# Up-projection of a decoder block: one written order for four engines instead of the scheduler's, and other buffers for operands and weights

## The chip, the cores and the metric

The kernel runs on one core of a Trainium2 chip. The metric is device time in microseconds (us) of the program. Before the change three runs gave 2145.63 us as their median (2145.47 to 2150.24); the run that was profiled took 2145.27 us. Engines are called as the profile calls them: PE (TensorE), PEld (its weight loads), DVE (VectorE), ACT (ScalarE), POOL (GpSimd) and SP (the queue that issues the DMAs).

## The reference, cut to what matters

One decoder layer in float32, 1024 tokens, model width 1024. The change lies in the first half of the feed-forward part:

```
x = layer_norm(ALPHA*x + mixed, ln1_g, ln1_b)          # x: 1024 x 1024
h = causal_dwconv(x @ w_up, conv_w, conv_b)            # w_up: 1024 x 5632; 3 taps over tokens
h_gate, h_val = split(h, 2)                            # 2816 columns each
ffn = (silu(h_gate) * h_val) @ w_down
```

Before it stand the token mixers and the first layer norm, behind it the down-projection and a last gated stage; they compute the same in both kernels.

## The kernel before, in words

A float32 product is made of three fp32r matmuls: each operand is split into a high part (`hi_of`, L101, on ACT) and the rest (`lo_of`, L106, on POOL or DVE), and `mm3` adds high x high, high x low and low x high (L155).

The up-projection takes the 44 blocks of 128 columns of `w_up` as 22 pairs: block f of the gate half and block f of the value half. For a pair, 256 columns times 1024 tokens, the 2x2 scheme with seven products is used (Strassen-Winograd): `left_operands` makes seven operands of the weights, called W0 to W6 here, with four additions or subtractions on DVE (L164), `right_operands` made the seven XS tiles of the tokens once, before the stage. Each product is 4 x 3 = 12 matmuls of 512 columns, so a pair has 84. Products land in four PSUM banks A to D and are put together by DVE (L1043) and ACT (L1050, L1074) into two halves `h`. The convolution of a half is one ACT instruction (L1085) and two taps on DVE (L1087); the gate half goes through Silu on ACT (L1089), POOL multiplies it with the value half (L164), and SP stores it to DRAM (L1097).

The weights of pair f+1 are made while pair f is multiplied. There is one buffer for each of the seven W (four in pool `wq`, three in `fp`), so W of the next pair waits until the product of the last pair is done with it. The raw weights of even pairs lie in `wr` tiles, of odd pairs in `ar` tiles.

What sets the order: the code of a pair is a list of steps (`p0, p1, late p6, p5, late conv0, p2, p3, p4, conv1`), and the framework's scheduler, which works through a modelled timeline, orders the instructions of each engine on that base. Each engine then takes its instructions strictly in that order, each waiting for semaphores. The other stages are ordered by the scheduler in both kernels.

The last pair's gate half (`last_conv`) is finished within the first preparations of the down-projection, which are `bank_sets` of weights (`wu`) and activations (`au`).

Of the kernel before, what the change touches and what calls it, by code (L numbers as in the profile page):

```python
# [8 lines left out]
F32 = mybir.dt.float32  # L9
F32R = mybir.dt.float32r  # L10
# [7 lines left out]
P = 128  # L18
L = 1024
# [21 lines left out]
def hybrid_block(ctx: ExitStack, tc: tile.TileContext, x, p, w_in, w_gate_up, b_gate, g_gla, w_gla,  # L41
# [48 lines left out]
    def nm(s):  # L90
        uid[0] += 1
        return f"{s}_{uid[0]}"
# [15 lines left out]
    def split(hi, lo, src, eh="A", el="V"):  # L108
        hi_of(hi, src, eh)
        lo_of(lo, src, hi, el)  # L110
# [104 lines left out]
    def quad(a):  # L215
        return a.rearrange("p (a b) -> p a b", b=P)
# [39 lines left out]
    def run(steps):  # L256
        for f in steps:
            f()
# [687 lines left out]
    segd, segk = ExitStack(), ExitStack()  # L946
    xpool = pool("xset", stack=segx)
    open_residual([x[t * P:(t + 1) * P, :] for t in range(NT)], 5)
    XS = [bpool.tile([P, 2, 4, HALF], F32R, name=nm("xs"), tag="B") for _ in range(4)]
    with ExitStack() as c1:  # L950
        lp = pool("ln1", stack=c1)
        gb1 = load_gb(lp, ln1_g, ln1_b)
        SPREAD, XE, XA = (1, 3), ('GVGVGVG', 'GVGVGVG', 'GGGVGGG', 'VVGVVGV'), ('VVVV', 'VVVV', 'VVVV', 'VVVG')

        def x_sets(i, xf):

            if i == 0:
# [40 lines left out]
    with ExitStack() as c1:  # L998
        psum_banks(c1, "d", ch=8)
        fp = pool("ffwork", stack=c1)  # L1000
        rawp = pool("raws", stack=segd, side="right")
        wk = pool("upwork", stack=segk, side="right")
        UE, UE0, US = 'GGGGGGG', 'VVGVVGV', 'VVVV'
        nset = [0]

        def blocks(f):

            return (NF + f, f) if f < NF - 1 else (f, NF + f)

        def w_sets(f):  # L1010
# [8 lines left out]
            W = []  # L1019
            for _ in range(7):  # L1020
                n = nset[0] % 7
                nset[0] += 1
                pl, nb = (wq, 4) if n < 4 else (fp, 3)
                W.append([pl.tile([P, 512], F32R, name=nm(x), tag=x, bufs=nb) for x in ("wh", "wl")])
            run(left_operands(raw[1][:, :512], raw[1][:, 512:], raw[0][:, :512], raw[0][:, 512:],
                              lambda j, src: split(*W[j], src, "A", (UE if f else UE0)[j]), US))
            return [[quad(t) for t in w] for w in W]

        def up(f):

            W = w_sets(f)
            st, out_ = {}, {}

            def prod(ps, j, start):
                for k in range(4):
                    mm3(ps, (W[j][0][:, k], W[j][1][:, k]), (XS[j][:, 0, k], XS[j][:, 1, k]), start and k == 0, k == 3,
                        not start)  # L1040

            def plus(out, a, b):
                V.tensor_tensor(out=out, in0=a, in1=quad(b), op=ALU.add)  # L1043

            def p0():
                st["A"] = bank("ch")
                prod(st["A"], 0, True)
                st["h"] = [wk.tile([P, L], F32, name=nm("h"), tag=f"h{i}", bufs=2) for i in range(2)]
                st["hv"] = [h.rearrange("p (a g q) -> p g a q", g=2, q=P) for h in st["h"]]
                S.activation(st["hv"][1][:, 0], quad(st["A"]), AF.Copy)  # L1050

            def p1():
                st["B"] = bank("ch")
                prod(st["B"], 1, True)
                plus(st["hv"][0][:, 1], st["hv"][1][:, 0], st["B"])

            def p5():
                st["C"] = bank("ch")
                prod(st["C"], 5, True)

            def p2():
                st["D"] = bank("ch")
                prod(st["D"], 2, True)

            def p3():
                prod(st["B"], 3, False)
                s1, u3 = st["hv"][1][:, 0], st["hv"][1][:, 1]
                plus(u3, s1, st["B"])
                plus(s1, u3, st["C"])
                plus(u3, u3, st["D"])  # L1070

            def p4():
                prod(st["A"], 4, False)
                S.activation(st["hv"][0][:, 0], quad(st["A"]), AF.Copy)  # L1074

            def p6():
                prod(st["D"], 6, False)
                o = st["hv"][0][:, 1]
                plus(o, o, st["D"])

            def conv(i):
                c = blocks(f)[1 - i]
                h = st["h"][i]
                o = out_[c // NF] = wk.tile([P, L], F32, name=nm("cv"), tag="cv", bufs=3)
                S.activation(o, h, AF.Identity, bias=cbias[:, c:c + 1], scale=cw[:, 2, c:c + 1])  # L1085
                for d in (1, 2):
                    V.scalar_tensor_tensor(o[:, d:], h[:, :L - d], cw[:, 2 - d, c:c + 1], o[:, d:], ALU.mult, ALU.add)  # L1087
                if c < NF:
                    S.activation(o, o, AF.Silu)  # L1089

            def conv1():
                conv(1)

            def conv0():
                conv(0)
                sums(out_[0], out_[0], out_[1], ALU.mult, "G")
                nc.sync.dma_start(d_act[f // 6][:, f % 6], out_[0])  # L1097
            return p0, p1, p5, p2, p3, p4, conv1, p6, conv0

        late = []  # L1100
        for f in range(NF):
            p0, p1, p5, p2, p3, p4, conv1, *rest = up(f)
            run([p0, p1, *late[:1], p5, *late[1:], p2, p3, p4, conv1])
            late = rest
        late[0]()
        last_conv = late[1]
    segx.close()
    sega.close()

# [7 lines left out]
    with ExitStack() as c1:  # L1117
# [251 lines left out]
```

## Time and profile before

| what | value |
|---|---|
| median of the runs | 2145.63 us |
| the profiled execution | 2145.27 us, its span 2143.6 us |
| PE busy | 2063.3 us (96%) |
| DVE busy | 1564.6 us (73%) |
| POOL busy | 1000.0 us (47%) |
| ACT busy | 846.0 us (39%) |
| up-projection, first to last matmul | about 1296 to 1736 us of the span |

The profile shows, for each engine, when an instruction ran, how long, how long the engine stood idle before it and what released it. An engine's share over the whole span says little here, since the stages differ; the stage is read in stretches of its own. A pair of the up-projection repeats with the same pattern from one pair to the next, so one pair shows nearly all.

### The profile page before, as it was taken

What the parts mean: (1) busy time and instruction counts of PE and PEld (TensorE: products, weight loads), DVE (VectorE), ACT (ScalarE), POOL (GpSimd) and SP (SyncE); (2) the same over time, 40 slices, a digit from 0 to 9 for tenths busy, and PEclk for the clock granted to TensorE, in tenths of its full rate; (3) what the DMA queues carried; (4) which work ended last, traced back from release to release, by engine and by line L of the source; (5) the groups of instructions that cost most, each with busy time, mean ns of one, the idle gap of its engine ahead of it and who ended that gap; (6) DMA issues with size and microseconds to landing.
All of it is one profiled execution on the core that took longest, in us unless ns stands there. A gap on an engine that the chain in (4) does not pass through costs nothing.

```text
span 2143.6 us, 32563 instructions
## 1 busy us (share of the span) xinstructions
PE 2063.3 (96%) x12210; PEld 1811.3 (84%) x12210; DVE 1564.6 (73%) x2742; ACT 846.0 (39%) x1540; POOL 1000.0 (47%) x832
## 2 busy tenths in 40 slices
PE   9999999999999999999999978999999979999997
PEld 8888899998988888887788976877777769989897
DVE  3589999999227888876234487777777788895965
ACT  4343312213126766675222244344344353342421
POOL 2423444535422121213231586776776684554753
PEclk9999999999999999999999998999999989999999
DMA  4322211211226686779766442222222134323222
GB/s 138 79 64 79 86 31 57 57 50 52 64 86 130 130 157 130 144 158 212 205 216 122 147 153 87 86 72 87 81 69 89 64 109 148 118 94 119 89 99 79
DMA packets 377566, 227.14 MB, mean 106 GB/s; under 512 B 189328, under 2 KB 351760, under 8 KB 377408
## 3 DMA queue, kind: packets, MB, share of 16 engines
q1 hardware_dynamic: 377408, 225.06, 38.7%
q8 instruction: 96, 1.57, 0.3%
q14 instruction: 62, 0.51, 0.1%
HBM read 146.37 MB, written 40.89 MB: 87 GB/s over the span
## 4 chain that ended last, share of the span: by engine, by line
PE 29%; DVE 9%; POOL 7%; issue 5%; DMA 3%; ACT 2%; SPq 0%; POOLq 0%; DVEq 0%; ACTq 0%
PE ch L155 16%; PE mm L155 13%; POOL wl L106 4%; DVE cv L1087 1%; DMA wr<-d_ob 1%; DVE cx L164 1%; DMA dr<-in_w_down_dram 1%; DVE h L1043 1%; ACT cv L1085 1%; DVE ar L164 1%; DVE wu L106 1%; DVE res_all L910 1%; DVE res_all L164 0%; DVE stats L933 0%; POOL lnmv L212 0%
## 5 line engine op out<-in xcount | busy, mean ns | idle before, releaser
L106 POOL TENSOR_TENSOR wl<-wr,wh 128x512 fp32r<-128x512 f32 x304 | 439.8, 1461 | 288.3 <-ACT wh L101 280.7
L155 PE MATMUL ch<-xs,wh 128*128 128x512 f32 x1232 | 384.8, 394 | 5.8 <-ACT wh L101 3.2
L155 PE MATMUL mm<-Ah,wh 128*128 128x512 f32 x832 | 332.1, 399 | 2.7 <-ACT wh L101 1.6
L155 PE MATMUL mm<-Al,wh 128*128 128x512 f32 x832 | 330.4, 397 | 0.3 <-POOL Al L106 0.3
L155 PE MATMUL mm<-Ah,wl 128*128 128x512 f32 x832 | 329.4, 396 | 0.0
L155 PEld LDWEIGHTS ch<-xs,wh 128*128 128x128 f32 x1232 | 231.5, 189 | 58.7 <-DVE h L1043 4.1
L103 POOL TENSOR_SCALAR wh<-wr 128x512 fp32r<-128x512 f32 x112 | 75.2, 674 | 381.1 <-PE mm L155 194.4
L155 PE MATMUL ch<-xs,wl 128*128 128x512 f32 x616 | 242.8, 395 | 6.8 <-POOL wl L106 6.7
L155 PE MATMUL mm<-wl,Ah 128*128 128x256 f32 x768 | 217.1, 284 | 5.2 <-POOL wl L106 5.1
L155 PE MATMUL mm<-wh,Al 128*128 128x256 f32 x768 | 215.8, 283 | 0.0
L155 PE MATMUL ch<-wu,au 128*128 128x256 f32 x1512 | 194.0, 292 | 22.5 <-DVE au L106 7.2
L155 PE MATMUL mm<-wh,Ah 128*128 128x256 f32 x768 | 213.2, 283 | 0.0
L1087 DVE SCALAR_TENSOR_TENSOR cv<-h,cw,cv 128x1023 f32<-128x1023 f32 x88 | 168.6, 1915 | 60.0 <-ACT cv L1085 58.5
L155 PEld LDWEIGHTS ch<-wu,au 128*128 128x128 f32 x1512 | 190.4, 199 | 25.9 <-DVE au L106 8.1
L101 ACT ACTIVATE wh<-wr 128x512 fp32r<-128x512 f32 (+1 forms) x201 | 120.5, 623 | 194.7 <-PE mm L155 81.6
L155 PEld LDWEIGHTS mm<-Ah,wh 128*128 128x128 f32 x832 | 156.7, 188 | 33.4 <-ACT wh L101 2.1
L155 PEld LDWEIGHTS mm<-Ah,wl 128*128 128x128 f32 x832 | 156.4, 188 | 33.0
L155 PEld LDWEIGHTS mm<-Al,wh 128*128 128x128 f32 x832 | 156.5, 188 | 30.7 <-POOL Al L106 0.8
L674 DVE MATCH_REPLACE8 score<-m,score 128x896 f32<-128x896 f32 (+3 forms) x192 | 166.5, 869 | 0.0
L673 DVE MAX8 m<-score 128x8 f32<-128x896 f32 (+3 forms) x192 | 163.6, 876 | 2.3 <-POOL score L480 2.1
L155 PEld LDWEIGHTS mm<-wl,Ah 128*128 128x128 f32 x768 | 145.1, 189 | 7.1 <-POOL wl L106 6.4
L155 PEld LDWEIGHTS ch<-xs,wl 128*128 128x128 f32 x616 | 116.5, 189 | 38.2 <-POOL wl L106 14.0
(269 smaller groups left out, 4328.4 us busy)
## 6 DMA issues: line engine op xcount, KB each, us to landing
wr<-in_w_in_dram SPq DMA_DIRECT2D x60, 512.0 KB, 3.8
wr<-in_w_up_dram SPq DMA_DIRECT2D x22, 512.0 KB, 3.9
ar<-in_w_up_dram SPq DMA_DIRECT2D x22, 512.0 KB, 4.0
d_act<-cv SPq DMA_DIRECT2D x22, 512.0 KB, 2.6
dr<-in_w_down_dram SPq DMA_DIRECT2D x12, 768.0 KB, 7.0
ar<-d_act SPq DMA_DIRECT2D x12, 768.0 KB, 5.1
d_tg<-tg SPq DMA_DIRECT2D x32, 256.0 KB, 2.0
wr<-in_w_out_dram SPq DMA_DIRECT2D x16, 512.0 KB, 3.6
```

The lines of the kernel that those rows point to most:

```text
L101: S.activation(dst, src, AF.Copy, scale=scale)
L103: (V if eng == "V" else G).tensor_scalar(dst, src, scale, 0.0, ALU.mult, ALU.add)
L106: done["GV"[eng != "G"]] = (G if eng == "G" else V).tensor_tensor(out=dst, in0=src, in1=hi.bitcast(F32), op=ALU.subtract)
L155: T.matmul(ps, lhsT=l, rhs=r, start=start, stop=stop, skip_group_check=more)
L164: (G if eng == "G" else V).tensor_tensor(out=out, in0=a, in1=b, op=op)
L673: V.max(m8, score[t])
L674: V.match_replace(score[t], m8, score[t], TAKEN)
L910: V.scalar_tensor_tensor(r[:, a:b], r[:, a:b], mv[:, 2:3], gb[1][:, a:b], ALU.mult, ALU.add)
L1043: V.tensor_tensor(out=out, in0=a, in1=quad(b), op=ALU.add)
L1085: S.activation(o, h, AF.Identity, bias=cbias[:, c:c + 1], scale=cw[:, 2, c:c + 1])
L1087: V.scalar_tensor_tensor(o[:, d:], h[:, :L - d], cw[:, 2 - d, c:c + 1], o[:, d:], ALU.mult, ALU.add)
```

## The change: what it does

Four engines (PE, DVE, ACT, POOL) get a written order. Every step of a pair has a time in a plan, in microseconds from the pair's start (`ON` = 2.72 for a product, `PAIR` = 7 x `ON` = 19.04 for a pair); the steps of all pairs are sorted by that time and issued in that order, with the scheduler told to keep it. SP's order is still the scheduler's. Instructions, shapes and engines stay as they were.

Two assignments of buffers change as well. XS 5, 2, 3, 4 now lie in pool `B` and XS 0, 1, 6 elsewhere (before: 0 to 3 in `B`); W 0, 5, 1, 2 lie in `wq` and W 3, 4, 6 in `fp` (before: W 0 to 3 in `wq`, 4 to 6 in `fp`). Each W still has one buffer of its own. The last pair's value half and gate half are convolved as before, the gate half still as `last_conv`.

The diff, cut (the table of plan times shown by two lines for each kind):

```diff
-    XS = [bpool.tile([P, 2, 4, HALF], F32R, name=nm("xs"), tag="B") for _ in range(4)]
+    XS = {j: bpool.tile([P, 2, 4, HALF], F32R, name=nm("xs"), tag="B") for j in (5, 2, 3, 4)}
...
-                XS.extend(apool[0].tile([P, 2, 4, HALF], F32R, name=nm("xs"), tag="A") for _ in range(2))
-                XS.append(xpool.tile([P, 2, 4, HALF], F32R, name=nm("xs"), tag="X"))
+                for j, (pl, tag) in enumerate(((apool[0], "A"), (apool[0], "A"), (xpool, "X"))):
+                    XS[(0, 1, 6)[j]] = pl.tile([P, 2, 4, HALF], F32R, name=nm("xs"), tag=tag)
...
+        ON = 2.72
+        PAIR = 7 * ON
...
+        def w_place(j):
+            pl, nb = (wq, 4) if j in (0, 5, 1, 2) else (fp, 3)
+            return [pl.tile([P, 512], F32R, name=nm(x), tag=x, bufs=nb) for x in ("wh", "wl")]
+        plan = []
+        def at_time(t, f):
+            plan.append((t, len(plan), f))
...
+        def plan_weights(f):
+            t0 = (f - 1) * PAIR
...
+            def hi(t, j, src):
+                def f_():
+                    w[j] = w_place(j)
+                    hi_of(w[j][0], r[src], "A")
+                at_time(t0 + t, f_)
+            def lo(t, j, src):
+                at_time(t0 + t, lambda: lo_of(w[j][1], r[src], w[j][0], "G"))
+            def comb(t, out, x, y, op):
+                at_time(t0 + t, lambda: sums(r[out], r[x], r[y], op))
+            at_time(t0 - 8.0, load)
...
+            comb(6.1, "11", "11", "21", ALU.subtract)
...
+            lo(15.0, 1, "22")
...
+        def plan_pair(f):
+            t0 = f * PAIR
...
+            def store():
+                sums(st["o", 0], st["o", 0], st["o", 1], ALU.mult, "G")
+                sent[0] = nc.sync.dma_start(d_act[f // 6][:, f % 6], st["o", 0])
...
+            prod(1, "B", 1)
+            plus(5.45, (0, 1), (1, 0), "B")
...
+            last = conv(0, PAIR + 9.0, PAIR + 10.3, PAIR + 13.4) + [(t0 + 2 * PAIR + 5.5, store)]
...
+        with tc.manual_schedule(engines={nc.tensor.engine, nc.vector.engine, nc.scalar.engine, nc.gpsimd.engine}):
+            for _, _, step in sorted(plan, key=lambda e: e[:2]):
+                step()
...
-            last_conv()
+            run(last_conv)
```

What this does to the queues is small in the middle of the stage. POOL, one round, before. `wl` is the low part of a W, `cv` the multiplication of the two halves; `ar` are the raw weights of the pair in hand (its last W is W6), `wr` those of the next pair in the order W0, W5, W1, W2, W3, W4:

```order
L106 TENSOR_TENSOR wl_2515_14755<-wr_2513_14752,wh_2514_14754 128x512
L106 TENSOR_TENSOR wl_2503_14623<-ar_2489_14608,wh_2502_14622 128x512
L106 TENSOR_TENSOR wl_2525_14765<-wr_2512_14750,wh_2524_14764 128x512
L164 TENSOR_TENSOR cv_2509_14698<-cv_2509_14698,cv_2487_14602 128x1024
L106 TENSOR_TENSOR wl_2517_14757<-wr_2512_14750,wh_2516_14756 128x512
L106 TENSOR_TENSOR wl_2519_14759<-wr_2512_14750,wh_2518_14758 128x512
L106 TENSOR_TENSOR wl_2521_14761<-wr_2513_14752,wh_2520_14760 128x512
L106 TENSOR_TENSOR wl_2523_14763<-wr_2513_14752,wh_2522_14762 128x512
```

The same round on POOL in the changed kernel (here `wr` is the pair in hand and `ar` the next):

```order
L106 TENSOR_TENSOR wl_2484_14526<-ar_2470_14443,wh_2483_14525 128x512
L164 TENSOR_TENSOR cv_2465_14422<-cv_2465_14422,cv_2453_14344 128x1024
L106 TENSOR_TENSOR wl_2488_14563<-wr_2446_14299,wh_2487_14562 128x512
L106 TENSOR_TENSOR wl_2492_14583<-ar_2469_14441,wh_2491_14582 128x512
L106 TENSOR_TENSOR wl_2496_14606<-ar_2469_14441,wh_2495_14605 128x512
L106 TENSOR_TENSOR wl_2498_14610<-ar_2469_14441,wh_2497_14609 128x512
L106 TENSOR_TENSOR wl_2500_14627<-ar_2470_14443,wh_2499_14626 128x512
L106 TENSOR_TENSOR wl_2504_14649<-ar_2470_14443,wh_2503_14648 128x512
```

The multiplication has moved two places up, from just ahead of W1's low part to just behind W0's. DVE in the same round, before (`ar` and `wr` rows are the four combinations of raw weights, the first for W6 of the pair in hand, the other three for the next pair; `h` are the sums with PSUM banks, `cv` the taps):

```order
L164 TENSOR_TENSOR ar_2345_13744<-ar_2345_13744,ar_2344_13742 128x512
L164 TENSOR_TENSOR wr_2369_13888<-wr_2369_13888,wr_2368_13886 128x512
L164 TENSOR_TENSOR wr_2368_13886<-wr_2368_13886 128x512
L1043 TENSOR_TENSOR h_2361_13791<-h_2362_13792,ch_2363_13794 128x4x128
L1043 TENSOR_TENSOR h_2337_13647<-h_2337_13647,ch_2342_13697 128x4x128
L1087 SCALAR_TENSOR_TENSOR cv_2365_13834<-h_2337_13647,cw_72,cv_2365_13834 128x1023
L1087 SCALAR_TENSOR_TENSOR cv_2365_13834<-h_2337_13647,cw_72,cv_2365_13834 128x1022
L164 TENSOR_TENSOR wr_2368_13886<-wr_2368_13886,wr_2369_13888 128x512
```

And in the changed kernel:

```order
L164 TENSOR_TENSOR ar_2326_13579<-ar_2326_13579,ar_2325_13577 128x512
L1111 TENSOR_TENSOR h_2365_13822<-h_2362_13803,ch_2361_13790 128x4x128
L164 TENSOR_TENSOR wr_2350_13723<-wr_2350_13723,wr_2349_13721 128x512
L164 TENSOR_TENSOR wr_2349_13721<-wr_2349_13721 128x512
L1111 TENSOR_TENSOR h_2341_13678<-h_2341_13678,ch_2346_13705 128x4x128
L1123 SCALAR_TENSOR_TENSOR cv_2369_13846<-h_2341_13678,cw_72,cv_2369_13846 128x1023
L1123 SCALAR_TENSOR_TENSOR cv_2369_13846<-h_2341_13678,cw_72,cv_2369_13846 128x1022
L164 TENSOR_TENSOR wr_2349_13721<-wr_2349_13721,wr_2350_13723 128x512
```

The first sum with a bank has moved up by two places; all else stands as it stood. At the stage's start, the last rows of DVE ahead of the first sum with a bank, before, where XS 1 is `xs_2057`:

```order
L106 TENSOR_TENSOR xs_2059_11730<-xq_2222_12993,xs_2059_11730 128x4x128
L164 TENSOR_TENSOR wr_2225_13042<-wr_2225_13042,wr_2226_13044 128x512
L106 TENSOR_TENSOR xs_2057_11728<-xq_2224_13000,xs_2057_11728 128x4x128
L164 TENSOR_TENSOR wr_2226_13044<-wr_2226_13044,wr_2225_13042 128x512
L106 TENSOR_TENSOR wl_2230_13049<-wr_2225_13042,wh_2229_13048 128x512
L106 TENSOR_TENSOR wl_2234_13053<-wr_2226_13044,wh_2233_13052 128x512
L106 TENSOR_TENSOR wl_2240_13059<-wr_2226_13044,wh_2239_13058 128x512
```

In the changed kernel, where XS 1 is `xs_2151`:

```order
L164 TENSOR_TENSOR wr_2226_13044<-wr_2226_13044,wr_2225_13042 128x512
L106 TENSOR_TENSOR xs_2152_12439<-xq_2224_13000,xs_2152_12439 128x4x128
L106 TENSOR_TENSOR xs_2058_11729<-xq_2222_12993,xs_2058_11729 128x4x128
L164 TENSOR_TENSOR xq_2224_13000<-xq_2224_13000,xq_2217_12972 128x512
L106 TENSOR_TENSOR wl_2240_13075<-wr_2226_13044,wh_2239_13074 128x512
L106 TENSOR_TENSOR xs_2151_12438<-xq_2224_13000,xs_2151_12438 128x4x128
```

XS 1, which the second product reads, has moved from the fifth place from the end to the last.

## Rows read from the trace of the kernel before

**Rows 1.** Busy time of each engine in stretches (us, instructions in brackets), granted clock.
```profile
core 0: us, PE busy (x) PEld busy (x) DVE busy (x) ACT busy (x) POOL busy (x), PEclk, DMA share, GB/s
1322.00:1398.00 76.00, 76.00 (x337) 62.91 (x336) 57.36 (x52) 32.10 (x47) 51.23 (x30) 1.00 0.25 77
1398.00:1736.00 338.00, 331.20 (x1430) 265.68 (x1429) 245.34 (x221) 140.16 (x205) 237.89 (x136) 1.00 0.25 80
1736.00:1746.00 10.00, 4.35 (x21) 3.27 (x19) 9.96 (x14) 7.94 (x16) 8.95 (x8) 0.77 0.03 10
```

**Rows 2.** Waits from 1300 to 1736 us: who for whom, us in total, times, longest.
```profile
PE ch L155 <- POOL wl L106: 6.7, 16, 0.6
```

**Rows 3.** PE in order of time: start, us, count; in brackets idle before and releaser.
```profile
1416.24 0.61 PE L155 MATMUL ch<-xs,wh 128*128 128x512 f32 x2
1416.69 0.39 PE L155 MATMUL ch<-xs,wl 128*128 128x512 f32 x1
1416.92 0.61 PE L155 MATMUL ch<-xs,wh 128*128 128x512 f32 x2
...
1419.41 0.61 PE L155 MATMUL ch<-xs,wh 128*128 128x512 f32 x2
1420.44 0.50 PE L155 MATMUL ch<-xs,wl 128*128 128x512 f32 x1 [0.41 <-POOL wl L106]
```

**Rows 4.** POOL in order of time, one round.
```profile
1436.60 2.41 POOL L164 TENSOR_TENSOR cv<-cv,cv 128x1024 f32<-128x1024 f32 x1 [2.37 <-issue]
1438.98 6.98 POOL L106 TENSOR_TENSOR wl<-ar,wh 128x512 fp32r<-128x512 f32 x4
1445.92 1.28 POOL L106 TENSOR_TENSOR wl<-wr,wh 128x512 fp32r<-128x512 f32 x1
1448.56 1.67 POOL L106 TENSOR_TENSOR wl<-ar,wh 128x512 fp32r<-128x512 f32 x1 [1.35 <-ACT wh L101]
1452.29 1.82 POOL L106 TENSOR_TENSOR wl<-wr,wh 128x512 fp32r<-128x512 f32 x1 [2.06 <-ACT wh L101]
1456.48 2.42 POOL L164 TENSOR_TENSOR cv<-cv,cv 128x1024 f32<-128x1024 f32 x1 [2.37 <-issue]
1458.85 1.29 POOL L106 TENSOR_TENSOR wl<-wr,wh 128x512 fp32r<-128x512 f32 x1
```

**Rows 5.** DVE in order of time, the same round.
```profile
1445.99 1.76 DVE L164 TENSOR_TENSOR ar<-ar,ar 128x512 f32<-128x512 f32 x1 [2.43 <-POOL wl L106]
1447.68 0.68 DVE L164 TENSOR_TENSOR wr<-wr,wr 128x512 f32<-128x512 f32 x1
1448.39 0.69 DVE L164 TENSOR_TENSOR wr<-wr 128x512 f32<-128x512 f32 x1
1449.00 1.28 DVE L1043 TENSOR_TENSOR h<-h,ch 128x512 f32<-128x512 f32 x2
1451.68 3.52 DVE L1087 SCALAR_TENSOR_TENSOR cv<-h,cw,cv 128x1023 f32<-128x1023 f32 x2 [1.40 <-ACT cv L1085]
1455.12 0.68 DVE L164 TENSOR_TENSOR wr<-wr,wr 128x512 f32<-128x512 f32 x1
1455.72 0.68 DVE L1043 TENSOR_TENSOR h<-h,ch 128x512 f32<-128x512 f32 x1
```

**Rows 6.** ACT in order of time, the same round.
```profile
1450.40 1.25 ACT L1085 ACTIVATE cv<-h,cbias,cw 128x1024 f32<-128x1024 f32 x1 [1.91 <-DVE h L1043]
1455.29 1.06 ACT L1089 ACTIVATE cv<-cv 128x1024 f32<-128x1024 f32 x1 [3.13 <-DVE cv L1087]
1456.26 1.13 ACT L101 ACTIVATE wh<-wr 128x512 fp32r<-128x512 f32 x2
```

**Rows 7.** The start of the stage: DVE and PEld in order of time.
```profile
1303.48 0.68 DVE L106 TENSOR_TENSOR xs<-xq,xs 128x512 fp32r<-128x512 f32 x1
...
1305.31 0.93 PEld L155 LDWEIGHTS ch<-xs,wh 128*128 128x128 f32 x3 [0.72 <-ACT xs L101]
...
1305.82 2.93 DVE L106 TENSOR_TENSOR wl<-wr,wh 128x512 fp32r<-128x512 f32 x2 [0.46 <-ACT wh L101]
```

**Rows 8.** PE's waits from 1730 to 1770 us.
```profile
PE ch L155 <- ACT au L101: 6.5, 1, 6.5
```

More of the change, by code (lines that the diff above doesn't have):

```diff
@@ L1002, in hybrid_block, with raw_weights @@
         wk = pool("upwork", stack=segk, side="right")
-        UE, UE0, US = 'GGGGGGG', 'VVGVVGV', 'VVVV'
-        nset = [0]
+        UE0, US = 'VVGVVGV', 'VVVV'
+        ON = 2.72
+        PAIR = 7 * ON
         def blocks(f):
             return (NF + f, f) if f < NF - 1 else (f, NF + f)
-        def w_sets(f):
+        def raw_weights(f):
             raw = []
@@ L1018, in w_sets @@
                 nc.sync.dma_start(raw[-1].rearrange("p (k c) -> p k c", k=KT), wup_v[:, :, c * P:(c + 1) * P])
[L1019 to L1081, printed above, removed]
@@ new lines, in raw_weights, with first_weights, put @@
+            return raw[1][:, :512], raw[1][:, 512:], raw[0][:, :512], raw[0][:, 512:]
+        def w_place(j):
[4 more added lines that the diff above has]
+            plan.append((t, len(plan), f))
+        W, ST, sent = {}, {}, [None]
+        def first_weights():
+            w = W[0] = {}
+            def put(j, src):
+                w[j] = w_place(j)
+                split(*w[j], src, "A", UE0[j])
+            run(left_operands(*raw_weights(0), put, US))
@@ new lines, in plan_weights, with load @@
+        def plan_weights(f):
+            w, r = {}, {}
+            t0 = (f - 1) * PAIR
+            W[f] = w
+            def load():
+                r.update(zip(("11", "12", "21", "22"), raw_weights(f)))
+            def hi(t, j, src):
+                def f_():
+                    w[j] = w_place(j)
+                    hi_of(w[j][0], r[src], "A")
[5 more added lines that the diff above has]
+            at_time(t0 - 8.0, load)
+            hi(3.3, 0, "11")
+            lo(3.9, 0, "11")
+            comb(6.1, "11", "11", "21", ALU.subtract)
+            comb(7.0, "21", "21", "22", ALU.add)
+            hi(11.0, 5, "22")
+            lo(11.6, 5, "22")
+            comb(13.3, "22", "22", "11", ALU.subtract)
+            hi(14.4, 1, "22")
+            lo(15.0, 1, "22")
+            hi(15.1, 2, "21")
+            lo(16.1, 2, "21")
+            hi(16.5, 3, "11")
+            lo(17.6, 3, "11")
+            hi(PAIR + 0.9, 4, "12")
+            lo(PAIR + 1.2, 4, "12")
+            comb(PAIR + 3.9, "12", "12", "22", ALU.subtract)
+            hi(PAIR + 8.3, 6, "12")
+            lo(PAIR + 8.9, 6, "12")
@@ new lines, in plan_pair, with prod, f_, half @@
+        def plan_pair(f):
+            t0 = f * PAIR
+            st = ST[f] = {}
+            def prod(n, ps, j):
+                def f_():
+                    start = ps not in st
+                    if start:
+                        st[ps] = bank("ch")
+                    wh, wl = (quad(t) for t in W[f][j])
+                    for k in range(4):
+                        mm3(st[ps], (wh[:, k], wl[:, k]), (XS[j][:, 0, k], XS[j][:, 1, k]), start and k == 0, k == 3,
+                            not start)
+                at_time(t0 + n * ON, f_)
+            def half(i):
+                if ("h", i) not in st:
+                    st["h", i] = wk.tile([P, L], F32, name=nm("h"), tag=f"h{i}", bufs=2)
+                return st["h", i]
+            def part(i, g):
+                return half(i).rearrange("p (a g q) -> p g a q", g=2, q=P)[:, g]
+            def copy(t, i, g, ps):
+                at_time(t0 + t, lambda: S.activation(part(i, g), quad(st[ps]), AF.Copy))
+            def plus(t, out, x, ps):
+                at_time(t0 + t, lambda: V.tensor_tensor(out=part(*out), in0=part(*x), in1=quad(st[ps]), op=ALU.add))
+            def conv(i, ta, tv, ts):
@@ L1082, in conv, with begin @@
                 c = blocks(f)[1 - i]
-                h = st["h"][i]
-                o = out_[c // NF] = wk.tile([P, L], F32, name=nm("cv"), tag="cv", bufs=3)
-                S.activation(o, h, AF.Identity, bias=cbias[:, c:c + 1], scale=cw[:, 2, c:c + 1])
+                def begin():
+                    o = st["o", c // NF] = wk.tile([P, L], F32, name=nm("cv"), tag="cv", bufs=3)
+                    S.activation(o, half(i), AF.Identity, bias=cbias[:, c:c + 1], scale=cw[:, 2, c:c + 1])
+                steps = [(ta, begin)]
@@ L1086, in conv @@
                 for d in (1, 2):
-                    V.scalar_tensor_tensor(o[:, d:], h[:, :L - d], cw[:, 2 - d, c:c + 1], o[:, d:], ALU.mult, ALU.add)
-                if c < NF:
[L1089 to L1098, printed above, removed]
@@ L1100, in hybrid_block, with tap_ @@
-        late = []
-        for f in range(NF):
[L1102 to L1106, printed above, removed]
+                    def tap_(d=d):
+                        o = st["o", c // NF]
+                        V.scalar_tensor_tensor(o[:, d:], half(i)[:, :L - d], cw[:, 2 - d, c:c + 1], o[:, d:], ALU.mult,
+                                               ALU.add)
@@ new lines, in conv @@
+                    steps.append((tv + 1.5 * (d - 1), tap_))
+                if c < NF:
+                    steps.append((ts, lambda: S.activation(st["o", 0], st["o", 0], AF.Silu)))
+                return [(t0 + t, s) for t, s in steps]
+            def store():
+                sums(st["o", 0], st["o", 0], st["o", 1], ALU.mult, "G")
+                sent[0] = nc.sync.dma_start(d_act[f // 6][:, f % 6], st["o", 0])
+            prod(0, "A", 0)
+            copy(2.8, 1, 0, "A")
+            prod(1, "B", 1)
@@ new lines, in plan_pair @@
+            plus(5.45, (0, 1), (1, 0), "B")
+            prod(3, "C", 5)
+            prod(4, "D", 2)
+            prod(5, "B", 3)
+            plus(16.3, (1, 1), (1, 0), "B")
+            plus(16.9, (1, 0), (1, 1), "C")
+            plus(17.5, (1, 1), (1, 1), "D")
+            prod(6, "A", 4)
+            copy(PAIR + 0.1, 0, 0, "A")
+            prod(9, "D", 6)
+            plus(PAIR + 8.2, (0, 1), (0, 1), "D")
+            last = conv(0, PAIR + 9.0, PAIR + 10.3, PAIR + 13.4) + [(t0 + 2 * PAIR + 5.5, store)]
@@ new lines, in plan_pair @@
+            for t, s in conv(1, 18.7, PAIR + 0.95, PAIR + 4.1) + (last if f < NF - 1 else []):
+                at_time(t, s)
+            return [s for _, s in last]
+        first_weights()
+        for f in range(NF):
+            if f:
+                plan_weights(f)
+            last_conv = plan_pair(f)
+        with tc.manual_schedule(engines={nc.tensor.engine, nc.vector.engine, nc.scalar.engine, nc.gpsimd.engine}):
+            for _, _, step in sorted(plan, key=lambda e: e[:2]):
+                step()
```

## The prediction

> **What bounds the kernel now.** I read first the busy time in stretches, to find where PE does not run through. Between 1322 and 1398 us it is busy all the time; from 1398 to 1736 us it is busy for 331 of 338 us, at a granted clock of 1.00 in both [rows 1]. In order of time PE starts three matmuls in 0.68 us (1416.24 to 1416.92), so the 84 of a pair need 28 x 0.68 = 19.04 us [rows 3]. The first stretch, 76 us, holds four pairs at just that; the second holds 17 pairs, 338/17 = 19.88 us each. So 0.84 us a pair is lost, about 14 us in all, 0.7% of the kernel, and that is the most the steady part can give. Nobody but PE's wait has to be looked for: it waits 16 times for POOL's `wl` [rows 2], each time at the same place, the first low part of the second product [rows 3], that is, for W1.
>
> What makes W1 late is seen on the other engines. W1's low part starts at 1438.98 and again at 1458.85 us, 19.87 us later [rows 4]: this is a loop, and I follow it once, with 0 at its start. POOL makes the low parts of W1 to W4: 0 to 6.98 [rows 4]. DVE's first combination waits for W4's and runs 7.01 to 8.77; the second and third, two sums with banks, the two taps (after ACT's start of the convolution, 1.25 us [rows 6]) and the fourth combination follow, up to 16.82 [rows 5]. Then ACT finishes Silu and makes W1's high part, which starts at 1456.26, is one of two in 1.13 us, and ends at about 17.9 [rows 6]. POOL, however, took up the multiplication at 1456.48 and is only free at 19.87 [rows 4]. DVE from the first combination on takes 9.8 us of the loop, the four low parts 7.0, and 3.05 lie between DVE's last combination and W1, some 2 of them because of the multiplication.
>
> The second thing to see is what POOL and DVE do to each other. A combination takes 0.68 us alone and 1.76 when W0's low part (1445.92 to 1447.20) began 0.07 us earlier: it ends 0.55 us behind it [rows 4, 5]. A low part takes 1.28 us alone and 1.67 when it comes during the third combination, ending 1.15 behind it [rows 4, 5]. So an instruction of either that reads two tiles of SBUF waits until the other's is done, and gains back 0.13 us of its own start. The sums with a bank do not take part: two ran in 1.28 us beside a low part, one of 0.68 beside the multiplication, which stayed at 2.42 [rows 4, 5].
>
> **The change part by part.** No instruction is added and none removed, so busy time stays; what moves is places in queues. In the steady part there are two moves that matter: POOL's multiplication goes from ahead of W1's low part to behind W0's, and DVE's first bank sum goes ahead of the second and third combinations. Walked with the durations above, 0 again at W1's low part:
>
> W1 to W4 on POOL, beside two taps as now, 0 to 6.98. First combination 7.01 to 8.77, behind W0's low part as now. The multiplication is issued at 8.2, waits for the combination and ends at 8.77 + 2.41 - 0.13 = 11.05. The bank sum, 8.7 to 9.4, is free. Second combination: issued 9.3, waits for the multiplication, ends 11.05 + 0.55 = 11.60 (before, it ran in 0.68). W6's low part waits for that and ends 11.60 + 1.15 = 12.75. Third combination waits for W6's: 12.75 + 0.55 = 13.30. Second bank sum to 13.9; ACT's start of the convolution 14.0 to 15.25; two taps with W5's low part between them, 3.52 as now, to 18.8; fourth combination to 19.4. ACT: Silu to 19.9, W1's high part 0.6 more, 20.45. POOL is idle and starts W1's low part at 20.5.
>
> So the loop gives 2 us back at the multiplication and pays 2.6 on DVE: the second combination 1.55 and the third about 1.0. It is 20.5 us instead of 19.87, still above PE's 19.04, and W1 remains what PE waits for. 16 further rounds (as many as the waits in [rows 2]) x 0.65 = 10.4 us. I take +10.5. Bounds for the two combinations' waits, from the nearest rows: nothing each, which leaves 18.2 us and PE as the bound, -14 us for the stage; or each behind one more low part of 1.28, +2.6 a round, far above. I take the walk, since every step in it has a row of the same pair of instructions. When the first late round comes I leave where it is (1398 us); two rounds earlier or later is 1.5 us each way.
>
> By the Trainium skill (SBUF — State Buffer, "Who interferes with whom") whichever of the two engines issues first holds the shared pair for its whole instruction and the other blocks fully. The rows agree but for the 0.13 us; taken without that, two handovers more in a round would make the sum 4 us higher. What speaks against the change in that rule is just what the walk shows: three SBUF combinations now stand beside POOL's longest instruction, where before two did not.
>
> The multiplication's new place puts behind it W6 and W5 of the same queue; their products come in the next pair, behind W1's at 20.5, so at about 24 and 27 on this scale, against low parts that are ready at 12.75 and by about 17.8: nothing. The changed kernel's ACT also waits for that multiplication to free a `cv` buffer (three in all) before it starts the convolution: done at 11.05 against 14.0, nothing. SP's loads of raw weights come at the same combinations as before, two to each round, and the share of the DMA engines is 0.25 [rows 1]: nothing.
>
> The start of the stage: the scheduler's order on DVE now has XS 1's low part last of the instructions ahead of the first bank sum, where it was fifth from the end. Product 1's second matmul needed it and others by 1305.31; DVE's last of these ended at 1305.82 + 2.93 = 1308.75, with 0.46 idle before [rows 7]. The same work in another order ends at about 1308, so product 1 starts 2 to 3 us later. I take +2.5; bounds 0 (POOL shares the tail differently) and +5 (two of them behind a low part of POOL besides, 1.76 instead of 0.68).
>
> The end: PE's long wait behind the stage is for ACT's `au`, 6.5 us [rows 8], while DVE is busy 9.96 of 10 us [rows 1]. DVE's list there is not shorter by the new buffers, and the last gate half is still finished among the preparations: 0, bounds -3 and +2.
>
> Sum: 2145.27 + 10.5 + 2.5 + 0 = 2158.3 us against the profiled run; the median of the runs is 0.36 us above that run, so about 2158.5.
>
> **Rivals.** (1) The plan holds as written and the loop falls below 19.04: the 14 us lost to waits go, -14 + 2.5, 2134 us. For it: the multiplication no longer stands before W1, and 2 us is more than the 0.84 lost. Against it: this needs 1.5 of the 2.5 us of new waits on DVE not to occur, and [rows 4, 5] show such a wait at each such meeting. It decides at a loop of 19.04.
> (2) One tie goes the other way: at 7.0 DVE's first combination gets in before W0's low part. Then it ends at 7.7, W0's at 8.85, the second combination waits for that only (9.4), the third for the multiplication (12.2), and W1 comes at about 19.4: 16 x -0.45 + 2.5 = -5, 2141 us, no difference that can be measured. Against it: in the same tie now POOL wins by 0.07 us [rows 4, 5].
> (3) Longer: a third meeting (W5's low part holds both taps, or the fourth combination), +1.28 a round: 16 x 1.9 + 2.5, about 2178 us. For it: DVE's slack is gone. Against: in the walk W5 falls between the taps, as now.
>
> **How the numbers follow.** The walk 0.74, rival 1 0.12, rival 2 0.09, rival 3 0.05. Differences under 0.3%, 6.4 us, are about what a measurement of this kernel cannot tell from none. The walk's own range is 2151 to 2166, from the bounds of the start and 0.3 us a round. Slower by over 0.3%: nearly all of the walk and rival 3, 0.78; within 0.3%: rival 2 and a little of the walk, 0.10; faster: rival 1, 0.12. The range, 2140 to 2170, takes in the walk and rival 2 and leaves out rivals 1 and 3.
>
> **What would show it.** In the changed profile: low parts of W1 20.4 to 20.7 us apart; the second combination at about 2.2 us and not 0.68, the third at 1.6 to 1.7; the multiplication at 2.8, directly behind W0's low part; POOL idle for over 2 us just ahead of W1's; PE waiting for W1's high part on ACT as well as for its low part on POOL, some 1.5 us a round; PE's long wait for `au` unchanged. If the second combination takes 0.68 us the prediction fails by its main term; if the pairs are 19.04 us long, rival 1 is right.

## The result, and the profile after

The changed kernel takes 2161.06 us (median of 4 runs, 2159.10 to 2164.76) against 2146.07 us for the kernel before on the same chip: a ratio of 1.0069, 95% interval 1.0055 to 1.0083. It is slower by 15.0 us; 12.9 were forecast. The profiled run took 2162.93 us (span 2161.2), 17.7 us more than that of before.

Busy time in stretches, as in [rows 1]: the first holds pairs 1 to 4, the second the late pairs.

```profile
core 0: us, PE busy (x) PEld busy (x) DVE busy (x) ACT busy (x) POOL busy (x), PEclk, DMA share, GB/s
1325.00:1402.00 77.00, 77.00 (x341) 63.83 (x340) 62.23 (x52) 31.80 (x46) 49.77 (x29) 1.00 0.24 76
1402.00:1750.00 348.00, 332.46 (x1426) 264.89 (x1426) 277.62 (x220) 141.10 (x207) 246.43 (x136) 1.00 0.24 77
```

PE now stands idle 15.5 us in the second stretch, where it was 6.8 us. DVE is busy 0.80 of it, against 0.73 in [rows 1], with as many instructions (220 and 221 in 17 pairs): they last longer. PE's waits from 1300 to 1770 us, beside [rows 2, 8]:

```profile
PE ch L155 <- POOL wl L106: 10.6, 17, 0.6
PE ch L155 <- ACT au L101: 6.1, 1, 6.1
PE ch L155 <- ACT wh L101: 5.0, 16, 0.3
```

To the wait for W1's low part one for its high part has come. PE in order of time, both at product 1, beside [rows 3]:

```profile
1504.38 0.73 PE L155 MATMUL ch<-xs,wh 128*128 128x512 f32 x2 [0.30 <-ACT wh L101]
1505.74 0.50 PE L155 MATMUL ch<-xs,wl 128*128 128x512 f32 x1 [0.63 <-POOL wl L106]
```

Now one round on POOL, DVE and ACT, which answers to [rows 4 to 6]; W1's low part opens the first row of POOL and the last:

```profile
1504.41 7.00 POOL L106 TENSOR_TENSOR wl<-wr,wh 128x512 fp32r<-128x512 f32 x4 [2.83 <-ACT wh L101]
1511.37 1.29 POOL L106 TENSOR_TENSOR wl<-ar,wh 128x512 fp32r<-128x512 f32 x1
1512.62 2.84 POOL L164 TENSOR_TENSOR cv<-cv,cv 128x1024 f32<-128x1024 f32 x1
1515.42 1.74 POOL L106 TENSOR_TENSOR wl<-wr,wh 128x512 fp32r<-128x512 f32 x1
1520.32 1.81 POOL L106 TENSOR_TENSOR wl<-ar,wh 128x512 fp32r<-128x512 f32 x1 [3.16 <-issue]
1524.96 2.53 POOL L106 TENSOR_TENSOR wl<-ar,wh 128x512 fp32r<-128x512 f32 x2 [2.83 <-ACT wh L101]
...
1511.44 1.76 DVE L164 TENSOR_TENSOR wr<-wr,wr 128x512 f32<-128x512 f32 x1 [1.18 <-POOL wl L106]
1513.13 0.68 DVE L1111 TENSOR_TENSOR h<-h,ch 128x512 f32<-128x512 f32 x1
1513.73 2.28 DVE L164 TENSOR_TENSOR ar<-ar,ar 128x512 f32<-128x512 f32 x1
1516.04 1.67 DVE L164 TENSOR_TENSOR ar<-ar 128x512 f32<-128x512 f32 x1
1517.63 0.67 DVE L1111 TENSOR_TENSOR h<-h,ch 128x512 f32<-128x512 f32 x1
1519.70 3.51 DVE L1123 SCALAR_TENSOR_TENSOR cv<-h,cw,cv 128x1023 f32<-128x1023 f32 x2 [1.39 <-ACT cv L1118]
...
1518.42 1.24 ACT L1118 ACTIVATE cv<-h,cbias,cw 128x1024 f32<-128x1024 f32 x1 [4.48 <-DVE h L1111]
```

The round is 1524.96 - 1504.41 = 20.55 us. Read it by the ends: the multiplication ends at 1515.46, the second combination (the 2.28) 0.55 behind it at 1516.01, W6's low part 1.15 behind that at 1517.16, the third combination (the 1.67) 0.55 behind that at 1517.71. A blocked instruction is not shown as idle: it shows as a long one, and its price is its length less the 0.68 of one that runs alone.

Where the 17.7 us of the profiled runs went: counted in stretches of 84 matmuls, a pair's, from the first product on, the second stretch starts 3.1 us later (1325.7 against 1322.5), the stage from there to its last matmul takes 11.0 us more (424.8 against 413.7), and what lies behind it 3.5 us more (410.8 against 407.3).

### The profile page after: what moved, and what is told of

Same layout as the page of the kernel before. It is cut to its first block, busy times and chain, and to the rows that moved or that the text cites. A ratio compares the mean times of both kernels' runs of the same rounds, so it can differ in the third digit from the quotient of the medians.

```text
span 2161.2 us, 32542 instructions
## 1 busy us (share of the span) xinstructions
PE 2069.9 (96%) x12210; PEld 1816.3 (84%) x12210; DVE 1602.7 (74%) x2742; ACT 847.0 (39%) x1540; POOL 1006.0 (47%) x832
## 4 chain that ended last, share of the span: by engine, by line
PE 22%; DVE 14%; ACT 7%; POOL 5%; issue 4%; DMA 2%; SPq 0%; DVEq 0%; POOLq 0%; ACTq 0%
PE mm L155 12%; PE ch L155 9%; POOL wl L106 3%; DVE cv L1123 3%; ACT wh L101 3%; DVE ar L164 2%; ACT cv L1118 2%; DVE wr L164 2%; DVE h L1111 1%; ACT h L1108 1%; DMA wr<-d_ob 1%; DVE cx L164 1%; DVE au L106 1%; DMA pt<-ab 1%; DVE wu L106 1%
## 5 line engine op out<-in xcount | busy, mean ns | idle before, releaser
L155 PE MATMUL ch<-xs,wh 128*128 128x512 f32 x1232 | 385.3, 394 | 10.6 <-ACT wh L101 5.0
L155 PE MATMUL ch<-xs,wl 128*128 128x512 f32 x616 | 243.4, 395 | 10.6 <-POOL wl L106 10.6
L1123 DVE SCALAR_TENSOR_TENSOR cv<-h,cw,cv 128x1023 f32<-128x1023 f32 x88 | 155.6, 1768 | 59.7 <-ACT cv L1118 58.2
L106 POOL TENSOR_TENSOR wl<-ar,wh 128x512 fp32r<-128x512 f32 x77 | 127.9, 1677 | 73.8 <-ACT wh L101 42.3
```

The costliest lines, as they stand in the source:

```text
L106: done["GV"[eng != "G"]] = (G if eng == "G" else V).tensor_tensor(out=dst, in0=src, in1=hi.bitcast(F32), op=ALU.subtract)
L155: T.matmul(ps, lhsT=l, rhs=r, start=start, stop=stop, skip_group_check=more)
L1123: V.scalar_tensor_tensor(o[:, d:], half(i)[:, :L - d], cw[:, 2 - d, c:c + 1], o[:, d:], ALU.mult, ALU.add)
```

## The experiments

The theory is the prediction's: W1 to W1 is a loop, and its length is what DVE and POOL make each other wait. Against it stand other causes: the place of the bank sum or of the multiplication alone, the buffers' new places, PE's order. Each ratio below is to the kernel before, run in turn with it on the same chip, where that took 2145.5 to 2146.8 us.

**1. The first bank sum back behind the combinations.**

```diff
-            plus(5.45, (0, 1), (1, 0), "B")
+            plus(7.6, (0, 1), (1, 0), "B")
```

> The first bank sum alone goes back behind the third combination; the multiplication stays behind W0's low part. Theory (a loop from W1's low part to W1's low part, in which the second and third combination wait for POOL's multiplication and for W6's low part): the combinations end at 11.6 and 13.3 us as in the changed kernel, since what they wait for does not move, but the bank sum's 0.6 to 0.7 us now stands behind them on the path: pairs 21.1 to 21.2 us, 2161 + 16 x 0.65 = 2171 us. Rival A (the sum put ahead of the combinations is the mistake, the multiplication's place is right): pairs at or under 19.9, 2150 us or less. Rival B (new buffer places or the order on PE cost the time): no change, 2161.

Measured: 2172.45 us, ratio 1.0124 (1.0107 to 1.0140). DVE, first combination to first combination, 21.16 us:

```profile
1498.14 1.76 DVE L164 TENSOR_TENSOR ar<-ar,ar 128x512 f32<-128x512 f32 x1 [1.19 <-POOL wl L106]
1499.82 2.88 DVE L164 TENSOR_TENSOR wr<-wr,wr 128x512 f32<-128x512 f32 x1
1502.73 1.66 DVE L164 TENSOR_TENSOR wr<-wr 128x512 f32<-128x512 f32 x1
...
1519.30 1.76 DVE L164 TENSOR_TENSOR wr<-wr,wr 128x512 f32<-128x512 f32 x1 [1.18 <-POOL wl L106]
```

The second combination is issued 0.6 us earlier, and waits 0.6 us longer: 2.88 instead of 2.28. The sum's time comes on top, as the theory says; rivals A and B fall. One thing the theory did not say: PE's wait changes its name. The product with W3 adds into the bank that the late sum still has to read, and from 1400 to 1760 us PE waits for nothing else:

```profile
PE ch L155 <- DVE h L1111: 23.1, 16, 1.9
```

**2. The multiplication back ahead of W1's low part.**

```diff
-            last = conv(0, PAIR + 9.0, PAIR + 10.3, PAIR + 13.4) + [(t0 + 2 * PAIR + 5.5, store)]
+            last = conv(0, PAIR + 9.0, PAIR + 10.3, PAIR + 13.4) + [(t0 + PAIR + 14.5, store)]
```

> The multiplication alone goes back to its place ahead of W1's low part; the first bank sum stays ahead of the second combination. Theory: POOL is again busy with it when W1's high part is ready (some 2 us), but W6's low part now follows W0's at once and the second combination, which is issued one bank sum later than in the kernel before, finds it running (1.65 instead of 0.68 us), and so does the third a low part; worked out step by step, 20.8 to 20.9 us a pair, 2161 + 16 x 0.3 = 2166 us. Rival A (the multiplication's new place is the whole loss): the pairs of the kernel before, 19.9, 2150 us. Rival B (buffer places, PE's order): no change, 2161.

Measured: 2165.43 us, ratio 1.0088 (1.0074 to 1.0103): about 4 us slower than the changed kernel, whose interval it touches. The time also holds a later start of the stage (experiment 6); the rounds show the loop alone: 20.77 us on DVE. The multiplication's old place, put back alone, does not bring the old time back. DVE, its three combinations and the first of the next round:

```profile
1497.76 1.76 DVE L164 TENSOR_TENSOR ar<-ar,ar 128x512 f32<-128x512 f32 x1 [2.43 <-POOL wl L106]
...
1500.04 0.68 DVE L164 TENSOR_TENSOR wr<-wr,wr 128x512 f32<-128x512 f32 x1
1500.75 1.66 DVE L164 TENSOR_TENSOR wr<-wr 128x512 f32<-128x512 f32 x1
...
1518.53 1.76 DVE L164 TENSOR_TENSOR wr<-wr,wr 128x512 f32<-128x512 f32 x1 [2.43 <-POOL wl L106]
```

The expectation had the second combination held by W6's low part and the third by another; the second went through in 0.68 and the third alone met W6's. That one meeting, 1.66 instead of 0.69 us [rows 5], is the whole 0.9 us a round over the kernel before; the size came out with half of the reason.

**3. Both bank sums ahead of the combinations.** What the walk asks for: let DVE and ACT do, while the second combination waits, all that needs no such turn.

```diff
-            plus(PAIR + 8.2, (0, 1), (0, 1), "D")
+            plus(PAIR + 5.7, (0, 1), (0, 1), "D")
```

> From the changed kernel, the second bank sum too goes ahead of the second and third combination. Theory: both sums and ACT's start of the convolution (1.25 us) then run while the combinations wait, and the taps follow the third combination at once: 20.5 - 0.6 - 1.25 = 18.6 us for the loop, under PE's 19.04, so PE sets the pair and its waits for W1 go: 2161 - 17 x 1.5 = 2135 us, faster than both kernels. Rival A (DVE then waits for PE's seventh product ahead of the combinations, and the loop only takes another way): pairs of 19.9 to 20.5, 2150 to 2161 us. Rival B (buffer places, PE's order): 2161.

Measured: 2135.67 us, ratio 0.9947 (0.9934 to 0.9959): 10.4 us faster than the kernel before, 25 faster than the changed one, by one number of the plan. POOL's multiplication, each 19.02 us, and DVE between:

```profile
1500.71 2.85 POOL L164 TENSOR_TENSOR cv<-cv,cv 128x1024 f32<-128x1024 f32 x1
...
1519.73 2.85 POOL L164 TENSOR_TENSOR cv<-cv,cv 128x1024 f32<-128x1024 f32 x1
...
1503.16 0.69 DVE L1111 TENSOR_TENSOR h<-h,ch 128x512 f32<-128x512 f32 x1 [1.27 <-PE ch L155]
1503.76 1.72 DVE L164 TENSOR_TENSOR ar<-ar,ar 128x512 f32<-128x512 f32 x1
1505.51 0.69 DVE L164 TENSOR_TENSOR ar<-ar 128x512 f32<-128x512 f32 x1
1506.12 3.63 DVE L1123 SCALAR_TENSOR_TENSOR cv<-h,cw,cv 128x1023 f32<-128x1023 f32 x2
```

The second combination still waits (1.72), now for W6's low part, and the third doesn't. The taps follow it without a gap (1.39 us stood before them in the changed kernel). Rival A is half true: DVE does wait for PE's seventh product, 1.27 us, but it lies where the second combination would else wait for the multiplication, which ends at 1503.56. PE runs through, from 1402 to 1725 us:

```profile
1402.00:1725.00 323.00, 323.00 (x1427) 267.54 (x1426) 257.19 (x219) 140.63 (x202) 216.72 (x134) 1.00 0.26 84
```

**4. Half of the multiplication.**

```diff
-                sums(st["o", 0], st["o", 0], st["o", 1], ALU.mult, "G")
+                sums(st["o", 0][:, :HALF], st["o", 0][:, :HALF], st["o", 1][:, :HALF], ALU.mult, "G")
```

> From the changed kernel; the multiplication is done for half of the columns only, which leaves that part of the output wrong. Theory: it takes 1.28 instead of 2.41 us, the second combination ends 1.1 us earlier and with it W6's low part, the third combination and all behind: 20.5 - 1.15 = 19.3 us or less, so PE is as good as never late: 2161 - 17 x 1.3 = 2136 to 2141 us. Rival A (the combinations wait for something else, and POOL, idle for 2.8 us in each pair, has time for the multiplication): no change, 2161. Rival B (buffer places, PE's order): 2161.

Measured: 2132.39 us, ratio 0.9935 (0.9922 to 0.9947). POOL, then DVE:

```profile
1502.11 1.74 POOL L164 TENSOR_TENSOR cv<-cv,cv 128x512 f32<-128x512 f32 x1
1505.42 1.30 POOL L106 TENSOR_TENSOR wl<-wr,wh 128x512 fp32r<-128x512 f32 x1 [1.57 <-ACT wh L101]
...
1503.22 1.18 DVE L164 TENSOR_TENSOR ar<-ar,ar 128x512 f32<-128x512 f32 x1
1504.43 0.69 DVE L164 TENSOR_TENSOR ar<-ar 128x512 f32<-128x512 f32 x1
```

The second combination goes from 2.28 to 1.18 with the length of the instruction that it waits for, and again ends 0.55 us behind it. The third has no meeting left, since W6's low part comes after it: the rounds are PE's (no wait of PE in them), where 19.3 us were expected at most. The time is 4 us under the lower end of the expectation, and 3 under experiment 3 with the same rounds, within the two intervals. POOL stood idle for 2.83 us a round in the changed kernel and had the time for that half, so it is not POOL's load that costs.

**5. Both sums ahead, the multiplication in its old place.** Experiment 3 with the edit of experiment 2.

> Both bank sums ahead of the second and third combination, and the multiplication back ahead of W1's low part: the fourth of the four ways to set these two moves. Theory: with the sums out of the way DVE's last combination is early enough, but POOL's multiplication again keeps W1's low part some time: pairs of 19.2 to 19.4 us, a little over PE's 19.04: 2135.7 + 16 x 0.25 = 2140 us. Rival A (with both sums ahead the multiplication's place is without effect): pairs 19.04, 2136. Rival B (its old place costs the 2 us seen before on W1): pairs over 20.5, 2160.

Measured: 2140.12 us, ratio 0.9976 (0.9965 to 0.9987). The time and the rounds are the theory's; rivals A (2136) and B (2160) fall. POOL again starts W1's low part from the multiplication and not from its high part, each 19.32 us:

```profile
1494.16 2.41 POOL L164 TENSOR_TENSOR cv<-cv,cv 128x1024 f32<-128x1024 f32 x1 [3.63 <-ACT cv L1127]
1513.48 2.41 POOL L164 TENSOR_TENSOR cv<-cv,cv 128x1024 f32<-128x1024 f32 x1 [3.63 <-ACT cv L1127]
1515.84 5.76 POOL L106 TENSOR_TENSOR wl<-ar,wh 128x512 fp32r<-128x512 f32 x3
```

With this all six ways to set the two moves have been measured; us from one round to the next:

| | multiplication ahead of W1 | behind W0's low part |
|---|---|---|
| both sums behind the combinations | 19.87 (kernel before) | 21.16 (experiment 1) |
| first sum ahead | 20.77 (experiment 2) | 20.55 (changed kernel) |
| both sums ahead | 19.32 (experiment 5) | 19.02, PE's own 19.04 (experiment 3) |

No run has the written order with both moves undone; the kernel before, with the scheduler's order and the old places of the buffers, stands for it. The moves don't add. The first sum's move costs 0.90 in the left column and gains 0.61 in the right one; the multiplication's costs 1.29 in the first row and gains in the two others.

**6. The buffers.** Old places for XS and W, with the changed kernel's order (first), and with both sums ahead besides (second):

```diff
-    XS = {j: bpool.tile([P, 2, 4, HALF], F32R, name=nm("xs"), tag="B") for j in (5, 2, 3, 4)}
+    XS = {j: bpool.tile([P, 2, 4, HALF], F32R, name=nm("xs"), tag="B") for j in (0, 1, 2, 3)}
...
-                    XS[(0, 1, 6)[j]] = pl.tile([P, 2, 4, HALF], F32R, name=nm("xs"), tag=tag)
+                    XS[(4, 5, 6)[j]] = pl.tile([P, 2, 4, HALF], F32R, name=nm("xs"), tag=tag)
...
-            pl, nb = (wq, 4) if j in (0, 5, 1, 2) else (fp, 3)
+            pl, nb = (wq, 4) if j in (0, 1, 2, 3) else (fp, 3)
```

> The changed kernel's order on every engine of the steady part, with the operands' and the weights' old places. Theory: the loop of W1 does not depend on where the tiles lie, so pairs stay at 20.5 to 20.6 us; only the start of the stage changes, where the scheduler's list on DVE follows the places: pair 1 starts 2.5 to 3.1 us earlier, 2158 us. Rival (the new places make a buffer come free later, and that holds W1): pairs of 19.0 to 19.9 us, 2133 to 2148 us.

> Both bank sums ahead of the second and third combination, with the operands' and weights' old places. Theory: two separate terms that add: pairs of 19.04, and pair 1 2.5 to 3.1 us earlier than in the changed kernel: 2135.7 - 3 = 2133 us. Rival (the places are needed for this order, since a buffer comes free too late in the old ones): pairs over 19.3 us, 2138 us or more.

Measured: 2156.37 us, ratio 1.0048 (1.0035 to 1.0061), and 2130.89 us, 0.9929 (0.9916 to 0.9941). Either is some 4 us under its fellow with the new places (10.9 against 15.0 us above the kernel before, 14.6 against 10.4 below), as both theories have it, by 2 us more than they say. The loop does not move, POOL, W1's low part to W1's low part, first run:

```profile
1480.75 7.00 POOL L106 TENSOR_TENSOR wl<-ar,wh 128x512 fp32r<-128x512 f32 x4 [2.83 <-ACT wh L101]
...
1501.30 6.99 POOL L106 TENSOR_TENSOR wl<-wr,wh 128x512 fp32r<-128x512 f32 x4 [2.83 <-ACT wh L101]
```

So the places are a term of their own, and a loss here. To find which, each was put back alone, the edits above one by one:

> From the changed kernel, the weights' old places alone (W0 to W3 in one pool, W4 to W6 in the other); XS keep the new ones. Theory of the prediction (XS 1's low part, last on DVE ahead of the stage, makes the start late): this alone leaves the start as it is, pair 1 at 1325, 2161 us. Rival (the late start is the scheduler's taking W0's combinations and low parts on DVE ahead of the last rows of the residual, which hangs on the weights' places): product 0 starts 3 us earlier and the time is 2157 to 2158 us. Pairs 20.5 to 20.6 us by both.

> From the changed kernel, the old places of XS alone; the weights keep the new ones. Theory of the prediction: XS 1's low part is not last any more, the start is 2 to 3 us earlier, 2158 us. Rival (the weights' places make the late start): about 1 us or nothing, 2160 to 2161 us. Pairs 20.5 to 20.6 us by both.

Measured: 2162.11 us, 1.0067 (1.0055 to 1.0080), with W's old places; 2160.46 us, 1.0062 (1.0049 to 1.0076), with those of XS. Neither alone brings the 4 us back beyond its interval. With W's old places the time is that of the theory, with those of XS that of the rival: by either run the places put back would not be the cause, and yet both together are. PE's first two products, the changed kernel first, then with W's old places:

```profile
1299.04 1.22 PE L155 MATMUL ch<-xs,wh 128*128 128x512 f32 x2 [2.59 <-DVE xq L164]
1306.31 0.49 PE L155 MATMUL ch<-xs,wh 128*128 128x512 f32 x1 [1.84 <-ACT xs L101]
1308.01 0.77 PE L155 MATMUL ch<-xs,wh 128*128 128x512 f32 x1 [1.21 <-DVE xs L106]
```

```profile
1299.72 1.22 PE L155 MATMUL ch<-xs,wh 128*128 128x512 f32 x2 [2.59 <-DVE xq L164]
1308.38 1.22 PE L155 MATMUL ch<-xs,wh 128*128 128x512 f32 x2 [3.61 <-ACT wh L101]
```

With XS's old places alone:

```profile
1296.06 1.22 PE L155 MATMUL ch<-xs,wh 128*128 128x512 f32 x2 [2.59 <-DVE xq L164]
...
1305.03 0.77 PE L155 MATMUL ch<-xs,wh 128*128 128x512 f32 x1 [1.20 <-DVE xs L106]
```

In the changed kernel product 1 waits for the low part of XS 1, as predicted. With W's old places it waits for a W instead, about as long and as late; with those of XS it still waits for XS 1, so that instruction's place in the list follows from W's buffers. Product 0, too, starts at another time in each, but the executions come to the stage up to 3.4 us apart. So the start is counted here from a matmul of the stage before, the 400th ahead of product 0 (1226.5 us in the kernel before, 1225.5 in the changed one); us in one execution each:

| | to product 0 | 84 matmuls further |
|---|---|---|
| kernel before | 69.1 | 96.0 |
| changed kernel | 73.5 | 100.1 |
| changed, W's old places | 72.1 | 100.1 |
| changed, XS's old places | 71.8 | 99.9 |
| changed, both old places | 69.0 | 97.2 |
| both sums ahead, new places (experiment 3) | 73.5 | 100.3 |
| both sums ahead, both old places | 70.1 | 97.4 |
| experiments 1, 2 and 4 | 75.0 to 75.1 | 101.7 to 103.2 |

The time is lost ahead of product 0, in the stage before, where the order is still the scheduler's: all of it in the changed kernel, 3.0 and 2.7 us with W's and with XS's old places. Either of the new places alone makes the start some 4 us late, both together make it no later, and only with both old ones do 3 us of it come back. With the new places of XS, 143 of PE's matmuls in the stage before stand in another order; with the old ones they stand as in the kernel before, but with the new places of W PE then waits longer there for DVE's rows of the residual (`res`, 12.8 us in three waits against 11.0). Why the scheduler orders them so is not shown. The last row shows that edits of the plan alone move the start as well, which is why the rounds carry the argument above, and not the times.

Behind product 0 nothing is lost: the 84 matmuls take 26.9 us in the kernel before and 26.6 in the changed one. Product 1's waits for XS 1 (1.84 and 1.21 us) have only taken the place of one for W1's high part, a row that [rows 2] leaves out; kernel before, from 1300 to 1736 us:

```profile
PE ch L155 <- ACT wh L101: 3.2, 1, 3.2
```

**7. The copy of the first bank, later.** On top of the second run of experiment 6:

```diff
-            copy(PAIR + 0.1, 0, 0, "A")
+            copy(PAIR + 5.1, 0, 0, "A")
```

> As the run with both bank sums ahead and the old places, and ACT's copy of the first bank, which only ACT's start of the convolution needs, 5 us later in the plan. Theory: pairs stay at PE's 19.04, the copy is beside PE's work, so the same 2133 us, at most 1.5 less where the stage ends. Rival (a later copy keeps the bank and PE waits for it): pairs over 19.04, 2137 us or more.

Measured: 2130.30 us, ratio 0.9928 (0.9915 to 0.9940), the same as without it. It and its fellow are the fastest versions here, 0.7% under the kernel before.

## Why the prediction was right, point by point

- **The bound.** Right: the first four stretches of 84 matmuls stay at PE's 19.04 us (no idle time up to 1402 us), and from there W1 is late in every round.
- **The main term.** Right in mechanism and size: the loop is 20.55 us (20.5 forecast), the second combination 2.28 (2.2), the third 1.67 (1.65), the multiplication 2.84 directly behind W0's low part (2.8), POOL idle 2.83 us ahead of W1 (over 2). 11.0 us against 10.5: the sum was short by the 0.05 us of a round, over the 16 late rounds. The late rounds begin at about 1402 us, as before.
- **Rivals.** Rival 1 (the loop falls below 19.04) did not occur here, for the reason given, and does occur when the meeting is shortened or filled (experiments 3 and 4). Rival 2's tie went to POOL by 0.07 us (1511.37 against 1511.44). Rival 3 needs W5's low part to hold both taps; they took 3.51.
- **The shared pair.** By the Trainium skill (SBUF — State Buffer, "Who interferes with whom") the engine that issues first holds the shared pair for its whole instruction, and the other blocks fully. The lengths of 2.28, 2.88 and 1.18 us follow it, but for the same small overlap as before: W6's low part ends 1.15 us behind the second combination, and takes 1.28 alone.
- **PE's waits** were put at 1.5 us a round; the view of waits shows (10.6 + 5.0)/16.5 = 0.95, though a round is 1.5 us longer than PE needs. The rest lies in matmuls shown as longer. For the price of a wait the distance from round to round is the safer reading, as it was in [rows 1, 2].
- **The start.** The number came out by luck, 3.1 us against 2.5; the step that gave it failed: "the scheduler's order on DVE now has XS 1's low part last of the instructions ahead of the first bank sum". PE does wait for that instruction, but loses nothing by it: in the kernel before it stood as long at the same product for W1's high part, 3.2 us, and from product 0 on both kernels take the same time (26.9 and 26.6 us). The loss lies ahead of product 0, in the stage before, where the prediction did not look (experiment 6).
- **Readings.** In [rows 5] the bank sum of 0.68 us "beside the multiplication" ended at 1456.40, before the multiplication began at 1456.48. That such a sum does not wait shows in the changed kernel: 0.68 us from 1513.13, with the multiplication running. Of the "three SBUF combinations" beside POOL's longest instruction only the second waits for it: the first holds it up, and the third waits for W6's low part. Without the two waits the walk leaves 17.9 us (20.5 less 2.6), not 18.2; PE would be the bound by both.
- **The end.** Forecast 0, 3.5 us in the profiled runs. PE's wait for `au` is as forecast (6.1 us, 6.5 before). The code behind it is the same in all of these kernels, whose profiled runs take 403.0 to 410.8 us for it, and PE's busy time for its 2938 matmuls goes along:

```profile
1765.00:2168.00 403.00, 364.97 (x2938) 358.76 (x2936) 316.25 (x525) 144.43 (x306) 224.78 (x189) 0.97 0.32 108
```

```profile
1750.40:2161.20 410.80, 369.68 (x2938) 363.90 (x2936) 318.40 (x525) 145.06 (x306) 223.75 (x189) 0.95 0.32 106
```

The first is experiment 1, the second the changed kernel; behind the stage every engine's instructions stand in the same order in both. Part of the difference goes with the granted clock, 0.97 and 0.95; the whole of it isn't explained by these columns, and since it varies among kernels with the same code it isn't put down to the change. The four runs of the changed kernel differ in the same manner: 2159.1 and 2159.2 us at a mean clock of 0.986, 2162.9 and 2164.8 at 0.983.

## What to carry to other kernels

An instruction that is moved out of a critical queue still runs somewhere: before counting what it gives back, look which instructions of the engine that it takes turns with (here POOL and DVE) stand beside it at the new place, and walk the loop on with the rows' durations, since busy shares show none of this. Where such a meeting can't be avoided, put into the wait what takes no part in it, here ACT's work and sums with one operand in PSUM (0.68 us also beside the multiplication). Measure such moves in all combinations: here the multiplication's move alone, the first sum's alone and the two together were each slower than neither, and with the second sum as well they were faster. A stage that the scheduler still orders can change with its neighbour's buffers: compare it, too, from an instruction that both kernels have in the same place.

## What the runs showed of the hardware that was not expected

In experiment 1 some rounds are longer than others. PE waits up to 1.9 us in a round there, and four times between 1390 and 1760 us its granted clock falls for a moment just behind such a wait; two stretches of 5 us:

```profile
1479.00:1484.00 5.00, 3.17 (x15) 2.31 (x13) 4.97 (x4) 0.47 (x1) 3.69 (x2) 1.00 0.64 215
1484.00:1489.00 5.00, 5.00 (x15) 3.96 (x16) 3.57 (x3) 1.76 (x2) 1.81 (x1) 0.66 0.34 100
```

PE stood idle for 1.8 us of the first stretch, and in the second the clock is 0.66, part of it at the lower level (1.2 GHz). In the changed kernel, with under 1 us of idle time a round, the clock stays at 1.00 from 1311 us to the end of the stage. The round with such a moment takes up to 22.8 us and the next one 19.5, and POOL's multiplications stay 21.13 to 21.19 us apart through it: here the slower PE cost nothing, since it was not the bound.
